# Low parts of the second halves of mixer weights: computed by GpSimd instead of VectorE

## The chip, the core and the metric

The kernel runs on one NeuronCore of one Trainium2 chip. The metric is device time in microseconds (us), as the median of several runs. One more execution was taken by the hardware profiler, and every trace row below comes from it. Engines are named as the profile names them: PE is TensorE's matmul stream, PEld its weight loads, DVE is VectorE, ACT is ScalarE, POOL is GpSimd, SP is the engine that queues the large loads.

## What is computed

Two layers (`DEPTH = 2`) on an input of 256 tokens by 1024 channels, all in float32. A layer norms x, projects it to four mixers (gated recurrence A, linear scan B, long convolution C, dilated attention D), merges the mixers' outputs through sigmoid gates, and ends with a gated feed-forward part:

```python
h = rmsnorm(x, norm1_g[l])
proj = h @ w_in[l]                       # 1024 x 4864: 19 blocks of 256 columns
pA, pB, pC, pD = jnp.split(proj, MIXER_OFFSETS, axis=-1)
...
for j, y in enumerate((yA, yB, yC, yD)):
    gate = jax.nn.sigmoid(h @ w_gate[l, :, j] + b_gate[l, j])
    mixed = mixed + gate * (y @ w_branch[l, j])
x = x + mixed @ w_out[l]
h2 = rmsnorm(x, norm2_g[l])
x = x + (jax.nn.silu(h2 @ w_ff1[l]) * (h2 @ w_ff3[l])) @ w_ff2[l]
```

## The kernel before

All weights lie in one array `wall[l, u]`, cut into 76 **units** per layer; a unit is 128 partitions by 2048 numbers and holds 256 columns of a projection. Units 0 to 18 are the mixers' input projections (`U_IN`), 19 to 34 the gates (`U_GATE`), 35 to 38 the branch projections, 39 to 42 the output projection, 43 and up the feed-forward part. Mixer A uses units 0 to 4 (3 is its value input), B 5 and 6, C 7 to 9, D 10 to 18 (16 is one of its value inputs).

A float32 product is made of three products of a faster 32-bit format: each factor is split into a high part (`hi`, the value rounded to that format) and a low part (`lo`, the value minus `hi`), and `mm3` (lines 142 to 144) issues high times high, high times low, low times high. `unit` (line 109) prepares a unit's two halves: SP loads `raw` (128x1024, line 124, 4 buffers), ACT makes `hi` by a copy (line 126, 6 buffers), DVE makes `lo` by a subtraction of two operands that both lie in SBUF (line 127, 5 buffers):

```python
with behind(*(then if hf and then else after)):
    SC.copy(hi, raw)
    V.tensor_tensor(lo, raw, hi.bitcast(F32), ALU.subtract)
```

In the trace and in the order lists, a name such as `lo_13_1_1709` is the low part of unit 13, half 1 (halves count from 0), with the allocation's number behind it. There are 304 such halves (two layers, 76 units, two halves).

`feat_unit` (line 146) multiplies one unit: 24 matmuls of 256 columns for each half, 8 of which read that half's `lo`. Between them PE runs the mixers' small products. Mixer A's core (line 541) is a chain of eight levels on DVE: at each level two products make `ab` (lines 570 and 571), PE turns it into scores `s` (line 549, 16 small matmuls, at the last level line 580), DVE merges them by a masked copy (line 584) and updates `U`, `W` and `T` (lines 612 to 614). Mixers B (scans, line 503), C (spectra, lines 674 to 700) and D (softmax, lines 753 to 814) also run on DVE and ACT between the weight splits.

POOL does little: it clears and loads the small weights of mixer B (`bw`, lines 460 and 462), sets `W` and `U` to one (line 521), builds the position bias by 48 small DMAs in layer 0 (`bias<-tab`, line 328), loads bias tiles (`bt`, line 753), the filter weights and the norm gains.

A scheduler places every instruction in the in-order list of its engine when the kernel is built, from a timeline of its own; `unit` asks for its work far ahead (`AHEAD`). So a change of one instruction's engine can reorder all five lists. An engine never overtakes within its list: if its next instruction waits, everything behind it waits too.

Of the kernel before, what the change touches and what calls it, by code (L numbers as in the profile page):

```python
# [8 lines left out]
F32 = mybir.dt.float32  # L9
# [3 lines left out]
ALU = mybir.AluOpType  # L13
# [13 lines left out]
U_IN, U_GATE, U_BR, U_OUT, U_FF = 0, 19, 35, 39, 43  # L27
# [16 lines left out]
def trunk(ctx: ExitStack, tc: tile.TileContext, A: dict, out: bass.AP, dbg=None):  # L44
    nc = tc.nc
    V, SC, G, PE = nc.vector, nc.scalar, nc.gpsimd, nc.tensor
# [56 lines left out]
    def behind(*ins):  # L103

        st = ExitStack()
        for i in ins:
            st.enter_context(tc.issue_after(i.ins))
        return st

    def unit(l, u, after=(), then=None, at=None):  # L110


        parts = []
        with tc.high_priority(offset=AHEAD):
            for hf in range(2):
                raw = wp.tile([P, 1024], F32, tag="raw", bufs=NRAW, name=f"raw{l}_{u}_{hf}")
                if at:
                    hi, lo = (get(f"{n}{l}_{u}_{hf}", F32R).rearrange("p a b -> p (a b)")
                              for n, get in zip(("hi", "lo"), at))
                else:  # L120
                    hi = wp.tile([P, 1024], F32R, tag="hi", bufs=NHI, name=f"hi{l}_{u}_{hf}")
                    lo = wp.tile([P, 1024], F32R, tag="lo", bufs=NLO, name=f"lo{l}_{u}_{hf}")
                with tc.issue_after(x_in.ins):
                    last_load[0] = nc.sync.dma_start(raw, A["wall"][l, u, :, hf * 1024 : hf * 1024 + 1024])
                with behind(*(then if hf and then else after)):
                    SC.copy(hi, raw)  # L126
                    V.tensor_tensor(lo, raw, hi.bitcast(F32), ALU.subtract)  # L127
                parts.append((hi, lo))
        return parts

# [313 lines left out]

    def mixer_b(l, h, after=()):
        ps = feat_unit(unit(l, 5, after if l else ()), h, f"bx{l}")
        xc = u2(f"bxc{l}")
        conv(ps, l, "lru_conv_w", 0, 4, 2, 2, "lru_conv_b", 0, xc)
        ps = feat_unit(unit(l, 6, after), h, f"bg{l}")
        t, gB = w2(f"bt{l}"), u2(f"bgl{l}")  # L450

# [59 lines left out]
    def mixer_a(l, h, v):  # L511
        sig = []
        kqe, kqo, U, W = (u4(f"{n}{l}") for n in ("kqe", "kqo", "U", "W"))
        ps = feat_unit(unit(l, 0), h, f"aq{l}")
        SC.copy(kqe[:, 2:4], ps)
        SC.copy(kqo[:, 2:4], ps)
# [655 lines left out]
```

## Time and profile before

| What | Value |
|---|---|
| Runs | 1003.1, 1000.2, 1001.65 us; median 1001.65 us |
| The profiled execution's own time | 999.49 us |
| Its span, first to last instruction | 997.6 us |
| PE busy | 976.9 us, 98% of the span |
| DVE busy | 655.4 us, 66% |
| ACT busy | 546.2 us, 55% |
| POOL busy | 48.1 us, 5% |
| Low parts on DVE (line 127) | 304 instructions, 1222 ns each on average |
| High parts on ACT (line 126) | 304 instructions, 1051 ns each on average |

The shares are means over stretches that have different limits; the granted clock was 0.999 of full speed over the span. Within a list an instruction's record overlaps the next one's by about 0.08 us, so 1222 ns of a low part costs DVE about 1.14 us from start to start.

### The profile page before, as it was taken

What the parts mean: (1) busy time and instruction counts of PE and PEld (TensorE: products, weight loads), DVE (VectorE), ACT (ScalarE), POOL (GpSimd) and SP (SyncE); (2) the same over time, 40 slices, a digit from 0 to 9 for tenths busy, and PEclk for the clock granted to TensorE, in tenths of its full rate; (3) what the DMA queues carried; (4) which work ended last, traced back from release to release, by engine and by line L of the source; (5) the groups of instructions that cost most, each with busy time, mean ns of one, the idle gap of its engine ahead of it and who ended that gap; (6) DMA issues with size and microseconds to landing.
All of it is one profiled execution on the core that took longest, in us unless ns stands there. A gap on an engine that the chain in (4) does not pass through costs nothing.

```text
span 997.6 us, 18829 instructions
## 1 busy us (share of the span) xinstructions
PE 976.9 (98%) x7770; PEld 913.2 (92%) x7770; DVE 655.4 (66%) x900; ACT 546.2 (55%) x815; POOL 48.1 (5%) x85
## 2 busy tenths in 40 slices
PE   7999999999999999999999999999999999999997
PEld 5889999999998999999989999999999889999996
DVE  6859894777766764455567679767667575555554
ACT  6696746545745544444457875554454464444442
POOL 0127200000000010000000000000000000000000
PEclk9999999999999999999999999999999999999999
DMA  8648455355555555555546445453465556555551
GB/s 286 202 133 217 135 170 171 116 170 159 183 174 164 187 169 190 188 186 180 186 148 210 162 158 160 158 177 106 163 228 173 170 161 211 187 182 189 187 172 43
DMA packets 51484, 172.41 MB, mean 173 GB/s; under 512 B 8716, under 2 KB 9413, under 8 KB 51398
## 3 DMA queue, kind: packets, MB, share of 16 engines
q1 hardware_dynamic: 47158, 163.41, 50.3%
q0 software_dynamic: 4240, 7.79, 3.1%
q8 instruction: 61, 1.00, 0.4%
q14 instruction: 25, 0.20, 0.1%
HBM read 170.08 MB, written 2.63 MB: 173 GB/s over the span
## 4 chain that ended last, share of the span: by engine, by line
PE 87%; DVE 5%; DMA 4%; ACT 2%; issue 1%; SPq 0%; DVEq 0%; ACTq 0%
PE f L142 9%; PE f L144 9%; PE f L143 8%; PE g L142 6%; PE g L144 6%; PE g L143 6%; PE acc L143 4%; PE acc L142 4%; PE acc L144 4%; DMA raw<-in_wall_dram 3%; DVE lo L127 2%; PE wo L143 1%; PE wo L144 1%; PE wo L142 1%; PE br L142 1%; PE br L143 1%
## 5 line engine op out<-in xcount | busy, mean ns | idle before, releaser
L127 DVE TENSOR_TENSOR lo<-raw,hi 128x1024 fp32r<-128x1024 f32 x304 | 370.2, 1222 | 223.0 <-PE f L143 109.5
L126 ACT CAST hi<-raw 128x1024 fp32r<-128x1024 f32 x304 | 317.5, 1051 | 294.3 <-PE f L144 99.8
L142 PE MATMUL f<-ahm,hi 128*128 128x256 f32 x640 | 181.1, 283 | 0.0
L144 PE MATMUL f<-alm,hi 128*128 128x256 f32 x640 | 181.1, 283 | 0.0
L143 PE MATMUL f<-ahm,lo 128*128 128x256 f32 x640 | 180.2, 282 | 0.0
L143 PEld LDWEIGHTS f<-ahm,lo 128*128 128x128 f32 x640 | 120.9, 189 | 1.0
L142 PEld LDWEIGHTS f<-ahm,hi 128*128 128x128 f32 x640 | 120.7, 189 | 0.9
L144 PEld LDWEIGHTS f<-alm,hi 128*128 128x128 f32 x640 | 120.4, 188 | 0.0
L142 PE MATMUL g<-ahi,hi 128*128 128x256 f32 x256 | 73.3, 286 | 2.1 <-ACT dvt L734 2.1
L144 PE MATMUL g<-alf,hi 128*128 128x256 f32 x256 | 72.8, 284 | 0.0
L142 PE MATMUL g<-ahf,hi 128*128 128x256 f32 x256 | 72.6, 283 | 0.2 <-ACT dvt L734 0.2
L143 PE MATMUL g<-ahf,lo 128*128 128x256 f32 x256 | 72.4, 283 | 0.0
L143 PE MATMUL g<-ahi,lo 128*128 128x256 f32 x256 | 72.3, 283 | 0.0
L144 PE MATMUL g<-ali,hi 128*128 128x256 f32 x256 | 72.3, 282 | 0.0
L143 PE MATMUL acc<-hi,fal 128*128 128x512 f32 x176 | 69.5, 395 | 0.0
L144 PE MATMUL acc<-lo,fah 128*128 128x512 f32 x176 | 69.3, 395 | 0.0
L142 PE MATMUL acc<-hi,fah 128*128 128x512 f32 x176 | 69.1, 395 | 0.0
L142 PEld LDWEIGHTS g<-ahi,hi 128*128 128x128 f32 x256 | 48.2, 188 | 3.3 <-ACT dvt L734 2.3
L142 PEld LDWEIGHTS g<-ahf,hi 128*128 128x128 f32 x256 | 48.2, 188 | 0.6 <-ACT dvt L734 0.4
L144 PEld LDWEIGHTS g<-alf,hi 128*128 128x128 f32 x256 | 48.2, 188 | 0.5 <-issue 0.3
L143 PEld LDWEIGHTS g<-ahi,lo 128*128 128x128 f32 x256 | 48.2, 188 | 0.2 <-issue 0.2
L143 PEld LDWEIGHTS g<-ahf,lo 128*128 128x128 f32 x256 | 48.2, 188 | 0.2 <-issue 0.2
(493 smaller groups left out, 2209.6 us busy)
## 6 DMA issues: line engine op xcount, KB each, us to landing
raw<-in_wall_dram SPq DMA_DIRECT2D x304, 512.0 KB, 4.6
bt<-bias POOLq DMA_DIRECT2D x8, 384.0 KB, 3.8
x<-in_x_dram SPq DMA_DIRECT2D x2, 512.0 KB, 6.1
bias<-tab POOLq DMA_DIRECT2D x16, 64.0 KB, 5.9
ngm<-in_norm_g_dram POOLq DMA_DIRECT2D x2, 512.0 KB, 4.3
out_dram<-x SPq DMA_DIRECT2D x4, 256.0 KB, 2.0
bias<-tab POOLq DMA_DIRECT2D x32, 16.0 KB, 4.3
ngf<-in_norm_g_dram POOLq DMA_DIRECT2D x1, 512.0 KB, 4.1
```

Of the source, the lines that this page charges most:

```text
L126: SC.copy(hi, raw)
L127: V.tensor_tensor(lo, raw, hi.bitcast(F32), ALU.subtract)
L142: PE.matmul(o, a[0], b[0], start=first, stop=False)
L143: PE.matmul(o, a[1], b[0], start=False, stop=False)
L144: return PE.matmul(o, a[0], b[1], start=False, stop=last)
```

## The change

The low part of a unit's second half (`hf` = 1) goes to POOL when the unit is below `U_GATE`, and in layer 0 at or above 12. These are units 12 to 18 in layer 0 and 0 to 18 in layer 1: 7 + 19 = 26 of the 304 subtractions. A blank line shifts the lines behind by one.

```diff
                 with behind(*(then if hf and then else after)):
                     SC.copy(hi, raw)
-                    V.tensor_tensor(lo, raw, hi.bitcast(F32), ALU.subtract)
+
+                    (G if hf and (0 if l else 12) <= u < U_GATE else V).tensor_tensor(lo, raw, hi.bitcast(F32), ALU.subtract)
                 parts.append((hi, lo))
```

All five lists are rearranged with it. Three places in layer 0 follow. In the lists `bt` is a bias tile, `s_1458` and `s_1459` are the scores of mixer A's last level, `ab_7_1455` their operand, `g` the product of a gate unit, `dv` that of unit 17.

POOL in layer 0, behind the bias DMAs, before:

```order
L328 DMA bias<-tab 64x1x256 x2
L328 DMA bias<-tab 64x1x64 x32
L753 DMA bt_2041<-bias 128x2x384
L753 DMA bt_2079<-bias 128x2x384
L753 DMA bt_2144<-bias 128x2x384
```

and after:

```order
L329 DMA bias<-tab 64x1x64 x8
L128 TENSOR_TENSOR lo_12_1_1645<-raw_12_1_1643,hi_12_1_1644 128x1024
L128 TENSOR_TENSOR lo_13_1_1709<-raw_13_1_1707,hi_13_1_1708 128x1024
L128 TENSOR_TENSOR lo_14_1_1774<-raw_14_1_1772,hi_14_1_1773 128x1024
L128 TENSOR_TENSOR lo_15_1_1837<-raw_15_1_1835,hi_15_1_1836 128x1024
L128 TENSOR_TENSOR lo_17_1_1901<-raw_17_1_1899,hi_17_1_1900 128x1024
L128 TENSOR_TENSOR lo_18_1_1963<-raw_18_1_1961,hi_18_1_1962 128x1024
L754 DMA bt_2041<-bias 128x2x384
```

Six low parts stand between the bias DMAs and the first bias tile; in layer 1 the 19 stand between the gain's load and the bias tiles, with mixer B's loads among them.

DVE in layer 0, the last levels of mixer A's chain, before:

```order
L612 TENSOR_TENSOR U_635<-U_635,T_4_1389 128x16x32
L127 TENSOR_TENSOR lo_24_0_2383<-raw_24_0_2381,hi_24_0_2382 128x1024
L613 TENSOR_TENSOR W_636<-W_636,T_4_1389 128x16x32
L571 TENSOR_TENSOR ab_6_1422<-U_635,kqo_634 128x8x64
L570 TENSOR_TENSOR ab_6_1422<-W_636,kqe_633 128x8x64
L584 COPY_PREDICATED Pc_1229<-masks,s_1396 128x256
L584 COPY_PREDICATED Pc_1230<-masks,s_1397 128x256
L612 TENSOR_TENSOR U_635<-U_635,T_5_1416 128x8x64
L127 TENSOR_TENSOR lo_24_1_2389<-raw_24_1_2387,hi_24_1_2388 128x1024
L613 TENSOR_TENSOR W_636<-W_636,T_5_1416 128x8x64
L571 TENSOR_TENSOR ab_7_1455<-U_635,kqo_634 128x4x128
L127 TENSOR_TENSOR lo_25_0_2447<-raw_25_0_2445,hi_25_0_2446 128x1024
```

and after:

```order
L613 TENSOR_TENSOR U_635<-U_635,T_4_1389 128x16x32
L614 TENSOR_TENSOR W_636<-W_636,T_4_1389 128x16x32
L128 TENSOR_TENSOR lo_18_0_1957<-raw_18_0_1955,hi_18_0_1956 128x1024
L572 TENSOR_TENSOR ab_6_1422<-U_635,kqo_634 128x8x64
L571 TENSOR_TENSOR ab_6_1422<-W_636,kqe_633 128x8x64
L585 COPY_PREDICATED Pc_1229<-masks,s_1396 128x256
L585 COPY_PREDICATED Pc_1230<-masks,s_1397 128x256
L613 TENSOR_TENSOR U_635<-U_635,T_5_1416 128x8x64
L614 TENSOR_TENSOR W_636<-W_636,T_5_1416 128x8x64
L572 TENSOR_TENSOR ab_7_1455<-U_635,kqo_634 128x4x128
L571 TENSOR_TENSOR ab_7_1455<-W_636,kqe_633 128x4x128
L128 TENSOR_TENSOR lo_23_0_2319<-raw_23_0_2317,hi_23_0_2318 128x1024
```

The low parts of the gate units (23 to 25) have moved behind the chain.

PE in layer 0, at the last level's scores, before:

```order
L144 MATMUL g_2329<-ali,hi_23_0_2318 128x256
L142 MATMUL g_2329<-ahi,hi_23_0_2318 128x256
L143 MATMUL g_2329<-ahi,lo_23_0_2319 128x256
L580 MATMUL s_1458<-ab_7_1455 128x128
L580 MATMUL s_1459<-ab_7_1455 128x128
```

and after:

```order
L144 MATMUL dv_1905<-ahi,lo_17_0_1895 128x256
L145 MATMUL dv_1905<-ali,hi_17_0_1894 128x256
L143 MATMUL dv_1905<-ahi,hi_17_0_1894 128x256
L581 MATMUL s_1458<-ab_7_1455 128x128
L581 MATMUL s_1459<-ab_7_1455 128x128
```

The same scores stand in the middle of unit 17 instead of unit 23. In PE's list of matmuls they stand 112 places further ahead than before; the scores of the last level in layer 1 stand 93 places further ahead.

## Rows read from the trace of the kernel before

**Rows 1.** The page's line of busy time, share of the span and instructions.

```profile
PE 976.9 (98%) x7770; PEld 913.2 (92%) x7770; DVE 655.4 (66%) x900; ACT 546.2 (55%) x815; POOL 48.1 (5%) x85
```

**Rows 2.** PE's waits: who for whom, us in total, times, longest.

```profile
PE f L142 <- ACT h2s L137: 3.3, 2, 2.1
...
PE g L142 <- ACT dvt L734: 2.3, 2, 2.1
...
PE s L549 <- DVE ab L570: 0.3, 1, 0.3
```

**Rows 3.** Busy time by engine in two stretches of mixer A's chain.

```profile
101.60:151.90 50.30, 48.22 (x575) 46.39 (x574) 48.20 (x76) 30.00 (x47) 4.05 (x7) 1.00 0.50 154
567.20:637.60 70.40, 69.61 (x788) 67.74 (x787) 62.73 (x97) 43.81 (x69) 0.00 (x0) 1.00 0.50 164
```

**Rows 4.** DVE timeline, ends of these stretches: start, us, instruction.

```profile
101.60 0.42 DVE L602 TENSOR_TENSOR T<-U 128x256 f32<-128x256 f32 x1
...
151.17 0.69 DVE L570 TENSOR_TENSOR ab<-W,kqe 128x512 f32<-128x512 f32 x1
...
567.20 0.69 DVE L570 TENSOR_TENSOR ab<-W,kqe 128x512 f32<-128x512 f32 x1
...
636.92 0.67 DVE L570 TENSOR_TENSOR ab<-W,kqe 128x512 f32<-128x512 f32 x1
```

**Rows 5.** Groups of DVE instructions by line and shape: busy us, mean ns, idle before.

```profile
L127 DVE TENSOR_TENSOR lo<-raw,hi 128x1024 fp32r<-128x1024 f32 x304 | 370.2, 1222 | 223.0 <-PE f L143 109.5 <-ACT hi L126 29.9 <-PE g L143 23.6
...
L584 DVE COPY_PREDICATED Pc<-masks,s 128x256 f32<-128x256 uint8 x24 | 9.2, 438 | 0.0
```

**Rows 6.** PE timeline around the scores of mixer A.

```profile
118.26 0.28 PE L144 MATMUL dk<-ali,hi 128*128 128x256 f32 x1
118.38 0.28 PE L142 MATMUL dk<-ahi,hi 128*128 128x256 f32 x1
118.59 0.69 PE L549 MATMUL s<-ab 64*64 64x64 f32 x32
119.22 0.39 PE L143 MATMUL dk<-ahi,lo 128*128 128x256 f32 x1
...
150.72 0.38 PE L142 MATMUL g<-ahi,hi 128*128 128x256 f32 x1 [2.08 <-ACT dvt L734]
...
153.31 0.38 PE L580 MATMUL s<-ab 64*128 64x128 f32 x2
...
638.07 0.49 PE L580 MATMUL s<-ab 64*128 64x128 f32 x4
```

**Rows 7.** POOL timeline: a series without a gap, and the end of the bias DMAs.

```profile
37.59 0.68 POOL L356 DMA_DIRECT2D hw<-in_hyw_dram  x1 [36.61 <-DVE sykb L338]
38.26 1.02 POOL L460 MEMSET bw<- 128x512 f32 x2
...
39.66 0.55 POOL L521 MEMSET U<- 128x512 f32 x1
...
103.73 2.44 POOL L328 DMA_DIRECT2D bias<-tab  x4 [0.52 <-DMA bias<-tab]
...
356.32 1.06 POOL L460 MEMSET bw<- 128x512 f32 x2 [55.99 <-PE fo L143]
```

**Rows 8.** DVE timeline: instructions beside POOL's series, and one of equal shape without it.

```profile
37.66 2.70 DVE L339 TENSOR_SCALAR sykb<-sykb 128x256 f32<-128x256 f32 x1
...
41.87 0.28 DVE L340 TENSOR_SCALAR sykb<-sykb 128x256 f32<-128x256 f32 x1
...
356.96 1.23 DVE L127 TENSOR_TENSOR lo<-raw,hi 128x1024 fp32r<-128x1024 f32 x1 [0.57 <-PE f L143]
```

**Rows 9.** Unit 16's second half in layer 0: high part, low part, first use (timelines).

```profile
14.45 1.07 ACT L126 CAST hi<-raw 128x1024 fp32r<-128x1024 f32 x1
...
17.41 1.21 DVE L127 TENSOR_TENSOR lo<-raw,hi 128x1024 fp32r<-128x1024 f32 x1
...
19.89 0.50 PE L144 MATMUL av<-lo,ahi 128*128 128x512 f32 x1
```

## The prediction

> **What bounds the kernel now.** I read the page's busy line first: PE is busy for 976.9 of 997.6 us [rows 1], so all of its idle time is 20.7 us, and no relief of another engine can be worth more. PE's waits say where a part of that lies [rows 2]: two waits for ACT's copy of `dvt` (2.1 us in layer 0, 0.2 in layer 1), 3.3 us for the filters' `h2s`, and 0.3 us for mixer A's `ab`. DVE is busy for 66% of the span, which looks like slack, but the mean hides two stretches. During mixer A's chain DVE is busy for 48.20 of 50.30 us in layer 0 and for 62.73 of 70.40 us in layer 1 [rows 3, 4]; POOL did 4 us in the first and nothing in the second. So DVE limits there, and PE, which has other projections to multiply meanwhile, is idle for 2.1 and 0.8 us in the same two stretches. These 2.9 us are what an earlier DVE could give back in the chains.
>
> **What is removed.** DVE loses 26 low parts. One record lasts 1222 ns [rows 5], of which about 0.08 us lies beside the next one, so 1.14 us each and 26 x 1.14 = 29.6 us of DVE. Only what falls into the two chains can reach PE; elsewhere PE does not wait for DVE.
>
> **What is moved.** The lists are rearranged as if the relief were real. In layer 0, up to the last product of the chain (`ab_7`), DVE's list is shorter by twelve low parts: the seven moved ones and five of gate units that now stand behind it, 12 x 1.14 = 13.7 us. In the trace that product ends at 151.17 + 0.69 = 151.9 us [rows 4], so it would end at 138.2 us. PE's list asks for it 112 matmuls sooner. Two matmuls start 0.12 us apart [rows 6], so that is 13.4 us; without the wait of 2.1 us before the gates, PE would come to these scores at 153.3 - 13.4 - 2.1 = 137.8 us. The two meet within 0.4 us: the new order leaves no reserve, and whatever delays DVE between 101.6 and 138 us is paid by PE one for one, because nothing overtakes in PE's list. In layer 1 PE asks 93 matmuls (11.2 us) sooner, at 638.1 - 11.2 - 0.5 = 626.4 us, or 59.2 us after the stretch began at 567.2. DVE's list there falls from 22 low parts to nine, so its work falls by 13 x 1.14 = 14.8 to 47.9 us: 11.3 us of reserve, of which the chain's own waits for PE and ACT took 70.40 - 62.73 = 7.7 us before.
>
> **What is added: the price on POOL.** No row shows POOL subtracting. The nearest rows are its clears of 512 numbers: three of them lie between the starts at 38.26 and 39.66 us [rows 7], 0.47 us each, so one stream of 1024 numbers takes 0.94 us. A subtraction has two streams in and one out; if the inputs come one after the other it takes 1.9 us, if all three do, 2.8 us. I take the middle, 2.3 us. A half unit keeps PE for 24 x 0.12 = 2.9 us and only each second half goes to POOL, so POOL's own rate (2.3 in 5.8 us) is no bound, and a latency that is 1.1 us longer is covered by five `lo` buffers, that is some 14 us of PE's work. [...]
>
> **What is added: who waits for POOL.** This is the term that decides. At 37.59 us POOL began a series of five instructions without a gap that ended at 39.66 + 0.55 = 40.2 us [rows 7]. DVE's L339, started at 37.66, took 2.70 us and ended at 40.4; an instruction of its shape with POOL idle took 0.28 us [rows 8]. So the two engines have something in common that one holds for as long as it works, and DVE stood still until POOL's whole series was through. It does not hold for every pair: a low part at 356.96 us, beside POOL's clear from 356.32 to 357.38, took 1.23 us as always [rows 7, 8]. But a clear reads nothing, whereas the new subtractions read two operands from SBUF at the same time as DVE's low parts, `ab`, `U`, `W` and scans read two. No row has that pair. From below the price is nothing (as at 356.96), from above the whole POOL instruction (as at 37.66). I take the upper case, because the row that shows it is the one in which both engines need the same direction of access, and the other row shows only that writing against reading is free. [...]
>
> **The sum.** Layer 0: five POOL subtractions (second halves of units 12, 13, 14, 15 and 17) fall between 106 us, where the bias DMAs end [rows 7], and 138 us. They hold DVE for at most 5 x 2.3 = 11.5 us. DVE's masked copies take their second operand from PSUM and can run beside them: twelve at 0.36 us (0.438 less the overlap) [rows 5] are 4.3 us, which leaves 7.2. I take 8 us; the bounds are 5 x 1.9 - 4.3 = 5.2 and 5 x 2.8 = 14. PE stalls for 8.4 (with the 0.4 above) and no longer for 2.1: +6 us. Layer 1: nine subtractions, 9 x 2.3 = 20.7 us, less 4.3 beside masked copies and less the reserve of 11.3 leaves 5.1; part of the reserve is waiting that POOL can use, part not. I take 3.5 and gain back 0.5: +3 us, bounds 0 and 12. The start: unit 16's second half of layer 0 has its high part at 15.5 us and is first used at 19.9 us [rows 9]; even at 2.8 us, and behind a low part of DVE until 16.6, POOL is done by 19.4, so I cost it at nothing. Around the first filters the lists change by a few places, and the waits there (part of the 3.3 us for `h2s`) may move by 1.5 us either way; I take 0. Mixer B's small weights in layer 1 are now loaded behind the sixth low part instead of at 356 us [rows 7], still before ACT's turn; 0, bound 2 us. The sum is +9 us. The profiled execution took 999.49 us, 1.9 more than its span; with +9 it would take 1008.5. The median of the runs is 2.2 us above it, so I forecast 1010.5 us.
>
> **Rivals.** First, the two engines do not disturb each other (the low part at 356.96 us is the model). Then DVE is on time, both stalls vanish, and 2.9 us come back: 998.8 us, 997 with luck at the start. For it speaks that row; against it that the reserve in layer 0 is 0.4 us even so. It decides by one point: the length of DVE's `lo` and `ab` between 106 and 138 us, 1.22 and 0.69 us in the trace before [rows 4, 5]. Second, POOL does hold DVE, but mostly in DVE's waits and beside operations that read PSUM: with the lower bounds, 5.2 + 0.4 - 2.1 in layer 0 and -0.5 in layer 1, some +3 us, and with luck at the start +1: 1003. Third, POOL itself is late: unit 12's low part stands behind 48 bias DMAs that ended at 106.2 us, and only with it does a `raw` buffer come free, on which SP's in-order loads wait. PE wants that low part near 120 us; if the bias DMAs ended 10 us later, each further microsecond would be PE's. It would add to the forecast: 1015 us. That the change does nothing is excluded: the lists show 26 subtractions on POOL.
>
> **How the numbers follow.** A measurement of this kernel can tell about 0.3%, 3 us, from no change, so faster means under 998.6 and slower over 1004.7. I give the forecast with its upper neighbours 0.58, the second rival 0.20, the first 0.22. Of the first a part stays above 998.6, since its whole gain is 2.9 us and only the start can add to it; of the second a part lies over 1004.7. That gives faster 0.18, within 0.24, slower 0.58. The range reaches from 997 (first rival) to 1018 (layer 0 without overlap, layer 1 at twice my value).
>
> **What would show it.** Right: POOL's subtractions last 2 us and more; DVE's `lo`, `ab`, `U` and `W` beside them grow by about as much; PE waits for `ab` at lines 549 and 580 for several us in both layers, and for nothing else that is new. Wrong: DVE's records keep their lengths, the waits for `dvt` and `ab` are gone, and the span falls to about 995. If PE instead waits at line 143 for low parts on POOL, the third rival holds.

## The result and the profile after

The changed kernel takes 1025.09 us (1024.06 to 1026.04) against 1000.92 us for the kernel before on the same chip: a ratio of 1.0254 with the interval 1.0238 to 1.027. The prediction was 1010.5 us with a range of 997 to 1018. The sign was right and the size too small by more than half. The profiled execution's span is 1022.9 us, 25.3 more than before.

The page's line of busy time (before: [rows 1]) and its row of TensorE's granted clock, in tenths, in 40 equal slices of the span:

```profile
PE 985.3 (96%) x7770; PEld 922.0 (90%) x7770; DVE 654.2 (64%) x874; ACT 542.2 (53%) x812; POOL 128.5 (13%) x111
...
PEclk9989989999999999999999998899999999999999
```

DVE lost 26 low parts and its busy time fell by 1.2 us, not by 29.6: sixteen of its instructions last longer than the same forms did before, by some 27 us in all. PE is idle for 1022.9 - 985.3 = 37.6 us (20.7 before), and it is busy for 8.4 us more with the same 7770 matmuls. These two differences, 16.9 and 8.4 us, are the 25.3 us.

PE's waits, as in [rows 2]:

```profile
PE s L550 <- DVE ab L571: 17.1, 6, 5.4
...
PE bz L143 <- ACT bxsh L138: 2.7, 1, 2.7
...
PE s L581 <- DVE ab L571: 2.1, 1, 2.1
PE f L143 <- ACT h2s L138: 1.9, 1, 1.9
```

The waits for `ab` went from 0.3 to 19.2 us; those for `dvt` are gone. The groups of low parts on both engines [rows 5]:

```profile
L128 DVE TENSOR_TENSOR lo<-raw,hi 128x1024 fp32r<-128x1024 f32 x278 | 344.9, 1243 | 227.8 <-PE f L144 109.9 <-ACT hi L126 27.6 <-PE g L144 21.9
...
L128 POOL TENSOR_TENSOR lo<-raw,hi 128x1024 fp32r<-128x1024 f32 x26 | 80.6, 3103 | 310.8 <-ACT xnf L206 212.3 <-ACT hi L126 35.6 <-DMA zd<-in_zT_dram 15.1
```

The mean on DVE hides what happens, and the mean on POOL mixes undisturbed instructions (2.40 us) with stretched ones. The longest wait of layer 1 shows it in order of time. DVE's timeline:

```profile
633.60 0.67 DVE L139 TENSOR_TENSOR dkl<-dk,dkh 128x512 fp32r<-128x512 f32 x1
634.21 2.28 DVE L571 TENSOR_TENSOR ab<-W,kqe 128x512 f32<-128x512 f32 x1
636.41 2.35 DVE L615 TENSOR_TENSOR T<-T 128x24 f32<-128x24 f32 x1
638.68 0.68 DVE L613 TENSOR_TENSOR U<-U,T 128x512 f32<-128x512 f32 x1
...
640.62 0.68 DVE L572 TENSOR_TENSOR ab<-U,kqo 128x512 f32<-128x512 f32 x1
641.23 3.36 DVE L128 TENSOR_TENSOR lo<-raw,hi 128x1024 fp32r<-128x1024 f32 x1
644.51 0.68 DVE L571 TENSOR_TENSOR ab<-W,kqe 128x512 f32<-128x512 f32 x1
```

POOL's timeline there:

```profile
626.60 12.12 POOL L128 TENSOR_TENSOR lo<-raw,hi 128x1024 fp32r<-128x1024 f32 x2 [8.77 <-DVE Pc L585]
641.05 2.46 POOL L128 TENSOR_TENSOR lo<-raw,hi 128x1024 fp32r<-128x1024 f32 x1 [2.33 <-ACT hi L126]
```

And PE, which meets the scores of this level:

```profile
640.47 0.28 PE L143 MATMUL dk<-ahf,hi 128*128 128x256 f32 x1
645.34 1.13 PE L550 MATMUL s<-ab 64*64 64x64 f32 x32 [4.59 <-DVE ab L571]
646.40 0.58 PE L144 MATMUL dk<-ahf,lo 128*128 128x256 f32 x1
```

`T` of 24 columns, an instruction of 0.17 us, lasts 2.35; the low part at 641.23 lasts 3.36 instead of 1.22 because POOL began one at 641.05. It is no part of the chain, but it stands in front of the second half of `ab` in DVE's list, and PE waits for that. POOL pays too: two subtractions that need 4.8 us alone take 12.12. And the matmuls' records after the wait are longer than before it (0.58, then 0.41, against 0.28). Stretches of 5 us of the same trace (columns as in [rows 3]; the value before the last two is the granted clock):

```profile
620.00:625.00 5.00, 4.24 (x47) 4.12 (x48) 5.00 (x10) 0.00 (x0) 0.00 (x0) 0.50 0.55 203
...
640.00:645.00 5.00, 0.75 (x7) 0.55 (x5) 5.00 (x6) 2.40 (x3) 2.46 (x1) 0.86 0.35 127
645.00:650.00 5.00, 4.66 (x65) 4.35 (x69) 5.00 (x11) 0.14 (x1) 0.00 (x0) 0.50 0.65 212
```

After the stall PE's granted clock reads 0.50 of full speed, and for a while matmuls of 256 columns start 0.21 us apart instead of 0.12. The stretches 50:55, 130:135 and 620:625 show 0.50 as well, each behind a wait of 2.7 to 5.4 us. In these four stretches PE is busy for 17.3 us; at the spacing before the waits that work would take 17.3 x 0.12 / 0.21 = 9.9 us, an estimate, so they account for some 7.4 of the 8.4 us of extra PE time. The stretches behind two of them still read 0.85 (55:60) and 0.84 (625:630).

### The profile page after: what moved, and what is told of

Its sections match the earlier page's. It is cut to its first block, busy times and chain, and to the rows that moved or that the text cites. A ratio compares the mean times of both kernels' runs of the same rounds, so it can differ in the third digit from the quotient of the medians.

```text
span 1022.9 us, 18877 instructions
## 1 busy us (share of the span) xinstructions
PE 985.3 (96%) x7770; PEld 922.0 (90%) x7770; DVE 654.2 (64%) x874; ACT 542.2 (53%) x812; POOL 128.5 (13%) x111
## 4 chain that ended last, share of the span: by engine, by line
PE 77%; DVE 4%; ACT 2%; DMA 1%; issue 1%; DVEq 0%; ACTq 0%
PE f L143 8%; PE f L145 8%; PE f L144 8%; PE g L145 5%; PE g L143 5%; PE g L144 5%; PE acc L144 4%; PE acc L145 4%; PE acc L143 4%; PE br L143 1%; PE wo L145 1%; PE wo L144 1%; PE wo L143 1%; PE br L145 1%; PE br L144 1%; DMA raw<-in_wall_dram 1%
## 5 line engine op out<-in xcount | busy, mean ns | idle before, releaser
L128 DVE TENSOR_TENSOR lo<-raw,hi 128x1024 fp32r<-128x1024 f32 x278 | 344.9, 1243 | 227.8 <-PE f L144 109.9
L128 POOL TENSOR_TENSOR lo<-raw,hi 128x1024 fp32r<-128x1024 f32 x26 | 80.6, 3103 | 310.8 <-ACT xnf L206 212.3
L145 PEld LDWEIGHTS g<-ali,hi 128*128 128x128 f32 x256 | 48.2, 188 | 0.4 <-issue 0.2
```

The costliest lines, as they stand in the source:

```text
L128: (G if hf and (0 if l else 12) <= u < U_GATE else V).tensor_tensor(lo, raw, hi.bitcast(F32), ALU.subtract)
L145: return PE.matmul(o, a[0], b[1], start=False, stop=last)
```

## The experiments

Ratios are to the kernel before, run on the same chip, with 95% intervals. "Place" is PE's place in its list where it asks for the scores of level 3 of mixer A's chain in layer 0, levels counted from 0 (936 before, 850 after). In acopy, amix256, pset and pcopy the subtraction of the 26 halves is left out.

| Kernel | What GpSimd does in the 26 places | Lists | Ratio |
|---|---|---|---|
| after | subtracts | new, place 850 | 1.0254 (1.0238 to 1.027) |
| l1only | subtracts, 19 in layer 1 | new in layer 1 | 1.0113 (1.0091 to 1.0136) |
| l0only | subtracts, 7 in layer 0 | new in layer 0 | 1.0117 (1.0087 to 1.0147) |
| acopy | nothing; ScalarE copies | new, place 908 | 0.997 (0.9957 to 0.9982) |
| amix256 | clears 3/4; ScalarE copies 1/4 | new, place 836 | 1.0032 (1.0015 to 1.0049) |
| pset | clears | new, place 827 | 1.0102 (1.0078 to 1.0126) |
| pcopy | copies | new, place 827 | 1.0146 (1.0107 to 1.0186) |
| dset2 | subtracts 8 columns and clears, unused | old, place 910 | 1.0018 (0.9998 to 1.0038) |
| dcopy | copies 2 x 448 columns, unused | old, place 921 | 1.0074 (1.0046 to 1.0103) |
| dhalf | subtracts 448 columns, unused | old, place 910 | 1.016 (1.0129 to 1.0191) |
| dsub | subtracts 2 x 448 columns, unused | old, place 910 | 1.0238 (1.0215 to 1.026) |

My theory was that GpSimd's subtractions hold VectorE in the chain; the main rival was that the new lists alone are too tight.

### Each layer alone

Of the condition only what differs is shown:

```diff
-(0 if l else 12) <= u < U_GATE     # after
+l and u < U_GATE                   # l1only
+not l and 12 <= u < U_GATE         # l0only
```

> Only layer 1's 19 low parts go to GpSimd; layer 0 keeps the lists of before, layer 1 has those of after. From the trace of after, the new gaps on PE in layer 1 are 4.3 and 4.8 us (behind 616.4 and 640.5 us), and part of the 8.4 us that PE lost at the lower granted clock follows them. If the loss is made in each layer by itself, this kernel is 9 to 13 us slower than before (1010 to 1014). If layer 1 only inherits a delay from layer 0, it is within 3 us of before.

> Only layer 0's seven low parts go to GpSimd. The new gaps on PE in layer 0 of after sum to 11.7 us around the scores and 2.9 us at the start, less the 2.1 us of the wait for dvt, with some 4 us of the lower clock: 14 to 18 us slower than before (1015 to 1019) if the layers are independent. By the rival, that layer 0's low parts are free in the shade of the bias DMAs and layer 1 makes the loss, within 4 us of before.

The two losses add up to that of after within their intervals (1.13 and 1.17% against 2.54%), so the layers lose each by itself, and alike. In the profiles PE's idle time grew by 8.2 us in the one and 10.1 us in the other, its busy time by 6.1 and 5.7.

### The relief without GpSimd

In the 26 places:

```diff
-G.tensor_tensor(lo, raw, hi.bitcast(F32), ALU.subtract)
+SC.copy(lo, hi.bitcast(F32))
```

> As after, but ScalarE writes the 26 low parts, by a copy of the high part (the subtraction of these halves is left out of the computation); GpSimd is idle as before. VectorE has the same relief, and in layer 1 the lists of PE and VectorE have the last level of the chain at the places of after (PE 4670 against 4669, VectorE 622 against 622); in layer 0 PE asks for it 57 places later than after and 55 sooner than before. Theory, the collision with GpSimd is the whole loss: no VectorE instruction is longer than in before, the waits for ab are under 2 us in all, 997 to 1002 us. Rival, the new lists alone are too tight: the waits for ab in layer 1 stay at 4 us or more, 1005 to 1012 us.

This is about what the change would be worth if GpSimd took the work at no price: 0.3%, 3 us. (Its list in layer 0 is 58 places looser than that of after.) VectorE's busy time is 626.6 us, 28.8 less than before. The stretch of layer 1's chain, from the first `ab` to the last, stands beside that of l1only, which asks for the levels there within a place of acopy's but for one (level 2, 26 places later in l1only). First PE's waits for `ab` in acopy, five of them in layer 1 and none over 0.63 us, then the stretch:

```profile
PE s L553 <- DVE ab L574: 2.1, 5, 0.6
...
566.00:626.70 60.70, 58.56 (x697) 56.86 (x695) 49.12 (x86) 46.83 (x70) 0.00 (x0) 1.00 0.46 157
```

and of l1only:

```profile
570.10:641.00 70.90, 62.11 (x687) 60.28 (x686) 58.77 (x84) 37.56 (x59) 30.13 (x9) 0.90 0.42 142
```

Up to the last `ab` VectorE makes nine low parts in both. In acopy it is busy for 49.12 us (0.07 of them in a tenth low part behind that `ab`); in l1only, beside nine low parts on GpSimd, for 58.77, and the chain lasts 70.9 us, as long as before with 22 low parts (71.0; [rows 3] begins 0.6 us later, at the second `ab`). The relief of the chain is given back as time in which VectorE is held, while PE's list, made for the relief, asks for the last level 93 places (11.2 us) sooner; so PE waits. The nine subtractions on GpSimd last 30.13 us, 3.35 each.

### The collision without the new lists

VectorE keeps all its work, and the lists are the old ones but for places in layer 0 ("old" in the table: level 3 asked for 15 to 26 places sooner, with two or three low parts fewer ahead of it; levels 4 and 5 up to 31 sooner, in dsub; the last level within one place, in dhalf 20 sooner). In layer 1 every level stands as before, on PE and on VectorE. GpSimd does something with the same operands that nobody reads.

```diff
 V.tensor_tensor(lo, raw, hi.bitcast(F32), ALU.subtract)
+if hf and (0 if l else 12) <= u < U_GATE:
+    for c in (slice(0, 448), slice(448, 896)):      # dhalf: the first alone
+        G.tensor_tensor(scratch, raw[:, c], hi.bitcast(F32)[:, c], ALU.subtract)
+        # dcopy: G.tensor_copy(scratch, hi.bitcast(F32)[:, c])
```

> The kernel before with VectorE still making all low parts and the lists of PE and VectorE as before, and beside it 26 groups of two unused subtractions on GpSimd (448 columns each, the same raw and hi as operands, result in a scratch tile that nobody reads) where after has its 26. Theory, contention: a GpSimd subtraction and a VectorE instruction with two SBUF operands hold each other; VectorE's records beside them grow by 1 to 2 us, and in the chain stretches, where VectorE was busy for 96% in layer 0, PE then waits for ab: 5 to 15 us slower than before (1007 to 1017). Rival, order: the loss of after is made by lists that leave no reserve, and contention is small; then this kernel, with the old lists, is within 3 us of before.

> As the run with unused subtractions, with one of 448 columns in place of two in each of the 26 places. Theory, VectorE and GpSimd share what they read with in turns, so the cost follows GpSimd's reading time once VectorE is saturated: about half of the 24.8 us, 1010 to 1015. Rival, each collision has a fixed price whatever its length: 1020 or more.

> The lists of before and, in each of the 26 places, two unused copies of 448 columns of hi on GpSimd (one operand read) instead of two unused subtractions (two operands). A copy of 1024 columns took 1.04 us on GpSimd against 2.40 for a subtraction, so GpSimd reads for 0.43 of the time. Theory, the cost follows the time in which GpSimd reads: 0.43 of 24.8, some 10 us, 1007 to 1014. Rival, only two operands collide: within 3 us of before. Rival, a fixed price for each collision: 1020 and more.

The collision alone, in nearly the old lists, costs as much as the whole change. (VectorE is not relieved there, so that the two are equal is chance.) The page of dsub, its waits for `ab`, and the stretch of layer 1's chain, from the first `ab` to the last:

```profile
PE 985.3 (96%) x7770; PEld 920.5 (90%) x7770; DVE 688.6 (67%) x900; ACT 545.5 (53%) x815; POOL 136.8 (13%) x137
...
PE s L553 <- DVE ab L574: 15.2, 5, 5.3
...
585.31:663.70 78.39, 70.23 (x779) 68.30 (x778) 74.80 (x98) 43.45 (x69) 30.46 (x18) 0.96 0.45 148
```

VectorE does the same 900 instructions in 33.2 us more. In layer 1, with every level at its old place, the chain takes 78.4 us instead of 71.0, and VectorE is idle in it for 3.6 us, less than before (7.7): its longer instructions make the delay, not buffers that GpSimd keeps for longer. Half of GpSimd's reading (dhalf) costs two thirds, 1.6%, a little over what I had expected. A copy reads one operand, took 0.56 us for 448 columns where a subtraction took 1.15, and costs a third (0.74%): one operand is enough to collide, and the price grows with GpSimd's reading, though not in proportion. The rivals "fixed price" and "two operands only" fall.

The control was to be clears, which read nothing. The first try did not tell:

> The lists of before, VectorE with all its work, and on GpSimd 26 series of five clears of an unused tile (448 columns each) where the run with unused subtractions had two subtractions. The control to that run: the same times of GpSimd's work, but nothing read. Theory, the collision needs a reading GpSimd instruction: within 2 us of before (998 to 1003), no VectorE instruction longer. Rival, GpSimd's mere work, its semaphores or the buffers that it keeps, made the 24.8 us: 1010 and more.

Its clears had no operand to wait for: 102 of the 130 ran before 80 us, the other 28 in one series at 103.2 to 118.0 us, and none in layer 1; the ratio is 0.9983 (0.9968 to 0.9997). With a subtraction of 8 columns ahead of each series they stay in place:

```diff
+    G.tensor_tensor(scratch[:, 0:8], raw[:, 0:8], hi.bitcast(F32)[:, 0:8], ALU.subtract)
+    for _ in range(5):
+        G.memset(scratch, 0.0)
```

> The clears of the earlier control had nothing to wait for and ran at the start of the program. Here each of the 26 series stands in its place: a subtraction of 8 columns of the same raw and hi, and five clears of 448 columns behind it, in the lists of before, VectorE with all its work. Theory, the price of GpSimd's work is the time in which it reads: the 8 columns cost some 0.1 us each, so within 3 us of before (997 to 1004), no VectorE instruction longer by over 0.5 us. Rival, any GpSimd work beside the saturated VectorE costs: 1010 and more, as with the unused subtractions.

No measurable cost, although PE asks for level 3 of layer 0 at the same place as in dsub (for levels 4 and 5 it asks 16 and 17 places later, and in layer 1 at the same places). GpSimd's timeline in the chain of layer 0:

```profile
128.02 2.69 POOL L130 TENSOR_TENSOR scratch<-raw,hi 128x8 bf16<-128x8 f32 x1 [12.14 <-ACT hi L127]
130.77 2.59 POOL L132 MEMSET scratch<- 128x448 bf16 x5
```

and VectorE's:

```profile
129.97 0.68 DVE L617 TENSOR_TENSOR U<-U,T 128x512 f32<-128x512 f32 x1
130.57 1.22 DVE L128 TENSOR_TENSOR lo<-raw,hi 128x1024 fp32r<-128x1024 f32 x1
131.71 0.68 DVE L618 TENSOR_TENSOR W<-W,T 128x512 f32<-128x512 f32 x1
```

Beside five clears (130.77 to 133.36) VectorE's two-operand instructions keep their lengths to the hundredth. The subtraction of 8 columns, 0.20 us elsewhere in this trace, lasted 2.69 beside VectorE's series of two-operand instructions. For the same 900 instructions VectorE is busy for 33.2 us more than before in dsub, 12.6 in dhalf, 7.3 in dcopy and 0.5 in dset2: the more GpSimd reads, the more VectorE loses.

### The new lists without a subtracting GpSimd

In the 26 places, one or two lines for each kernel:

```diff
-G.tensor_tensor(lo, raw, hi.bitcast(F32), ALU.subtract)
+G.memset(lo.bitcast(F32), 0.0)               # pset, behind ScalarE's copy
+SC.copy(lo[:, 0:256], hi.bitcast(F32)[:, 0:256])    # amix256, both lines
+G.memset(lo.bitcast(F32)[:, 256:1024], 0.0)
+G.tensor_copy(lo, hi.bitcast(F32))           # pcopy
```

> As after, but GpSimd only clears the 26 low parts (a memset, behind the same ScalarE copies; the subtraction of these halves is left out of the computation): it writes and reads nothing. Lists in layer 1 as after; in layer 0 PE asks for the last scores 81 places sooner than in after. If only a reading GpSimd instruction holds VectorE: no longer VectorE instruction, layer 1 free of stalls, 997 to 1004 us (the last 4 for layer 0's sooner scores). If writing holds it too: VectorE instructions longer by up to 1 us each, the whole near the 1015 us of the one-operand copies.

(GpSimd writes there, and reads nothing.)

> As after, but of each of the 26 low parts ScalarE writes a quarter by a copy and GpSimd clears the other three quarters (the subtraction of these halves is left out of the computation). GpSimd reads nothing, so by the run of the clears it holds nothing. In layer 0 PE asks for the last scores 18 places sooner than in after (994 against 1012), with VectorE's product at place 216 against 218; in layer 1 at the places of after. Theory, the lists of after are sound and the collision makes nearly all of the loss: waits for ab under 3 us in both layers, 997 to 1001 us. Rival, in layer 0 the new list of PE is too early by itself: waits for ab of 5 us or more there and a stretch at the lower clock, 1004 to 1010 us.

> As after, but GpSimd writes the 26 low parts by a copy of the high part (one operand read in place of two), so the subtraction of these halves is left out of the computation. In layer 1 the lists of PE and VectorE have the last level of mixer A's chain at the same places as after (PE 4669 against 4669, VectorE 622 against 622); in layer 0 PE's scores stand 73 places further ahead than in after. Contention by two operands on both sides: the low parts and ab of VectorE keep 1.2 and 0.7 us, layer 1 loses nothing, layer 0 at most 73 x 0.12 = 9 us: 998 to 1007 us. Rival, order: the stalls in layer 1 are there as in after (9 us), the whole near 1015 to 1025. Rival, any reading GpSimd instruction blocks: as after, a little less for a shorter instruction.

In layer 1, where pset asks for every level at the places of after, PE's longest waits for `ab` are 0.56 and 0.65 us (amix256: 0.73 and 0.71) against 4.10 and 4.59 in after: there the collision makes the loss. PE at level 2 and at level 5, in pset:

```profile
616.40 0.69 PE L553 MATMUL s<-ab 64*64 64x64 f32 x32
...
634.83 0.69 PE L553 MATMUL s<-ab 64*64 64x64 f32 x32 [0.23 <-DVE ab L574]
```

In layer 0 my theory is only half the truth. The rows of amix256, PE and then two stretches of 5 us:

```profile
118.12 0.28 PE L147 MATMUL dk<-ahi,hi 128*128 128x256 f32 x1
123.96 1.13 PE L554 MATMUL s<-ab 64*64 64x64 f32 x32 [5.57 <-DVE ab L575]
```

```profile
120.00:125.00 5.00, 1.04 (x32) 0.94 (x32) 5.00 (x11) 0.62 (x1) 0.00 (x0) 0.54 0.31 105
125.00:130.00 5.00, 5.00 (x57) 4.84 (x57) 5.00 (x13) 1.34 (x3) 0.00 (x0) 0.78 0.01 3
```

VectorE is busy throughout, no instruction of it in the chain of layer 0 is longer than before, and PE still waits 5.57 us for level 3, since its list asks for it 100 places sooner than before. In pset, at place 827, PE's waits around the scores of layer 0 (three for `ab`, one for a low part) sum to 8.0 us and the kernel loses 1%; in acopy, at 908, none for `ab` is over 0.3. After stands between (850), so a part of its loss in layer 0 is the list's; from these neighbours I estimate some 4 us of its 5.4 us of wait for level 3. Its own rows give less: two held instructions ahead of that `ab` (2.88 us at 107.71, 2.81 at 120.58) are 4.3 us too long, and PE would have come 0.9 us sooner, which leaves some 2 us. No kernel has the list of after in layer 0 without a reading GpSimd, so the split is not settled. In pcopy both act: the list is as early as in pset, and the one-operand copies held a dozen instructions of VectorE, by 9.2 us in all.

### Three more

```diff
+for c in range(0, 1024, 256):                             # psub4
+    G.tensor_tensor(lo[:, c : c + 256], raw[:, c : c + 256], hi.bitcast(F32)[:, c : c + 256], ALU.subtract)
+hf and not l and U_FF + 2 <= u < U_FF + 28                # ffn: condition
+hf and u != 16 and (0 if l else 12) <= u < U_GATE         # no16: condition
```

> As after, with each of the 26 subtractions on GpSimd cut into four of 256 columns; the lists stand as in after (PE 1016 and 4669 against 1012 and 4669). Theory, the two engines take turns instruction by instruction: no VectorE instruction is held by more than 0.8 us, but more of them are, and GpSimd stands behind one VectorE low part between its pieces; the time that both need stays the same, so 1018 to 1027 us. Rival, the loss comes from the 2.4 us for which single instructions of the chain stand still: it falls to a half or less, 1005 to 1013.

Ratio 1.0224 (1.0197 to 1.0251): nearly as slow. VectorE in psub4's layer 1, and GpSimd:

```profile
610.52 1.75 DVE L132 TENSOR_TENSOR lo<-raw,hi 128x1024 fp32r<-128x1024 f32 x1
612.20 1.21 DVE L576 TENSOR_TENSOR ab<-U,kqo 128x512 f32<-128x512 f32 x1
613.33 1.21 DVE L143 TENSOR_TENSOR dql<-dq,dqh 128x512 fp32r<-128x512 f32 x1
```

```profile
606.38 9.88 POOL L130 TENSOR_TENSOR lo<-raw,hi 128x256 fp32r<-128x256 f32 x8 [6.47 <-ACT hi L126]
```

Every instruction of the series is some 0.53 us longer while GpSimd does its eight pieces in 9.88 us: the engines alternate. Short pieces spread the price and hardly lower it (1.0224 against 1.0254).

> The 26 second halves that go to GpSimd are those of 26 units of layer 0's feed-forward part (units 45 to 70) instead of the mixers' units; there VectorE is busy for half of the time. GpSimd and VectorE collide there as often. Theory, a held VectorE costs time only where VectorE limits: within 3 us of before (997 to 1003). Rival, each collision delays the supply of weights and PE pays: 1005 us and more.

Ratio 1.0029 (1.0017 to 1.0042). In the feed-forward part seven of VectorE's low parts are held (six last 2.02 us, one 2.70, instead of 1.22), and PE waits for none of them. The small loss goes with 331 to 343 us, where layer 1's filters are finished on VectorE and three instructions were held by 2.1 us each; PE waited soon after for `hpm` (0.9 us) and `fhl` (1.7). In this kernel a collision costs where PE waits for VectorE, and nothing where it does not.

> As after without unit 16 (24 instead of 26 subtractions on GpSimd). In after PE's list asks for the first product of mixer B's gates (bz) 28 places sooner than before and waits 2.7 us for it; here it stands at its old place. If unit 16's move made that wait, it is gone, and the time is 2 to 4 us under after (1021 to 1023); in layer 0 PE asks for the last scores 45 places sooner than in after, which may take some of it back. If the wait has another cause, 1025.

1.0251 (1.0227 to 1.0274), no gain, though the wait for `bz` is back at 0.6 us. PE's waits for `ab` at line 550 rose to 19.1 us. Without the wait ahead of a stretch that VectorE limits PE waited longer in that stretch. But the list of no16 also asks for the last scores of layer 0 45 places sooner than that of after, so that the wait costs nothing by itself is not shown.

## Why the prediction was wrong in size

- **What the relief is worth: right.** I took 2.9 us at most; acopy gave 3.0 (1.8 to 4.3). The first rival's 998.8 us is near acopy's 997.78.
- **The price of a subtraction on POOL: right.** 2.3 us taken, 2.40 measured where VectorE is quiet.
- **That the engines exclude each other: right, by a row that does not show it.** L339 [rows 8] is a one-operand instruction, held beside a DMA issue and four clears (2.70 us instead of 0.28). Two-operand instructions kept their lengths beside clears (1.22 and 0.68 us in dset2 and pset), so the two rows of [rows 8] differed in VectorE's instruction, not in "the same direction of access". That the row led to the right term was luck. In pset the only instruction held in the stretches with the new clears was again of one operand (`U<-sf` 0.96 us instead of 0.43). The pair that no row of before had was in after: `ab` beside a GpSimd subtraction lasted 2.28 us instead of 0.68, `T` 2.35 instead of 0.17; a low part beside clears (dset2) lasted 1.22, as always. That the price would lie near the upper case was right.
- **The cost also runs the other way: not in the sum.** POOL waits for VectorE as well, so a subtraction of 2.40 us alone lasted 7.72 and two lasted 12.12.
- **Layer 1, +3 us: the step that failed most.** l1only measured +11.3 (9.1 to 13.6). I had counted 11.3 us of reserve from VectorE's work, 47.9 us against PE's call at 59.2. The work was right (49.12 in acopy, with the same nine low parts), but the chain takes 60.7 us even with nothing in its way, because VectorE is idle in it for 60.70 - 49.12 = 11.6 us, not the 7.7 of before, and PE waits for `ab` by 0.2 to 0.6 us at five levels even so. The reserve was nothing. The held time was 58.77 - 49.12 + 0.07 = 9.7 us, less than my 20.7 - 4.3 = 16.4, so two errors in part cancelled.
- **Layer 0, +6 us: also short.** l0only measured +11.7 (8.7 to 14.7). I compared the lists at the last level alone. At level 3 PE asks 86 places (10.3 us) sooner and VectorE's list is shorter by seven low parts (8.0 us); before, `ab` was ready there at 131.2 us and asked for at 132.9, so nothing of that 1.7 us is left before any collision. amix256, 14 places sooner still, waits 5.57 us there without one. That masked copies can run beside a subtraction, which took 4.3 us off my sum in each layer, no row of before showed; in after the two at 147.37 us lasted 0.77 us, as without GpSimd, inside a subtraction that lasted from 145.74 to 149.69 us.
- **TensorE's clock: no term, put at nothing without a reason.** Four waits of 2.7 to 5.4 us were each followed by a stretch at 0.50 granted, and PE's busy time grew by 8.4 us, a third of the loss.
- **The start at nothing: right in effect.** A wait for `bz` of 2.7 us came that I had not seen, since PE asks for it 28 places sooner; no16 was without it and gained nothing, with a tighter list behind it. The loads of `bw` cost nothing visible.
- **The third rival, POOL too late: no.** PE waited 0.7 us for a low part, at line 144, once, and that one was DVE's.
- **What would show it.** Of the signs given for "right" most came: POOL's 2.40 us, the longer `lo`, `ab` and `U`, and the waits for `ab` at line 549 (now 550). At line 580 (now 581) PE waited in layer 0 alone, 2.1 us; "nothing else that is new" was not so (`bz`); and the prediction had no sign for the clock.

## What to carry to other kernels

Before work goes to GpSimd to relieve VectorE, ask whether both will read SBUF at the same time: here a subtraction that costs VectorE 1.14 us took 2.40 us on GpSimd and held single instructions of VectorE by up to 2.2 us, while beside clears a low part kept its 1.22 us; so in a stretch where VectorE is saturated the move can give back all that it relieves. When lists are rearranged, compare the asking and the asked engine at every level of a chain, and take a chain's reserve from its end to end time and not from the busy time of one engine. Price a stall of TensorE with the slower stretch behind it: here four waits of 2.7 to 5.4 us were followed by stretches at 0.50 granted, and PE was busy for 8.4 us more.

## What the runs showed of the hardware that I had not expected

- The exclusion works both ways: a subtraction of 8 columns on GpSimd took 2.69 us beside VectorE's series instead of 0.20 (dset2). With pieces of 256 columns the engines took turns, +0.53 us on each VectorE instruction (psub4).
- One operand read by GpSimd is enough to hold VectorE (dcopy: low parts of 1.57 instead of 1.22 us, `ab` of 1.04 instead of 0.68), clears are not: beside them only one-operand instructions of VectorE were longer (0.96 instead of 0.43 us in pset).
- After waits of 2.7 to 5.6 us TensorE's granted clock read 0.50 to 0.54 in the next stretch of 5 us or in the stretch itself, in after, l1only and amix256. Behind a wait of 2.1 us for `dvt` it stayed at 1.00 in the kernel before (150 to 155 us) and fell to 0.50 in dset2 (151 to 154 us), so the length of a wait alone does not tell.
